# Rotary embedding on one core: slabs of one batch and 16 KB rows in place of slabs of two batches and 32 KB rows

## The chip, the cores and the metric

The kernel runs on one core of a Trainium2 chip. The metric is the device time of one execution in microseconds (us), as the median of several runs. Beside it there is a profile: one execution recorded by the hardware profiler, with every instruction and every DMA packet.

## What is computed

A rotary position embedding. `x` has 16 batches, 512 positions and 1024 columns in float32; the columns are 16 heads of 64, and each head is a first and a second half of 32. `cos` and `sin` have one row of 32 numbers for each position, shared by all batches and heads.

```python
x = x.reshape(batch, seq, num_heads, head_dim)
x1, x2 = x[..., :half_dim], x[..., half_dim:]
rotated = np.concatenate([x1 * cos - x2 * sin,
                          x1 * sin + x2 * cos], axis=-1)
```

32 MB (33.55 million bytes) are read and as many are written.

## The kernel before

**Slabs.** The work is cut into slabs of `nb` = 2 batches, 8 in all. A slab is 4 MB; each of the 128 partitions holds `rpp` = 8 consecutive positions, which are `W` = 8192 float32 numbers, one unbroken row of 32 KB both in HBM and in SBUF. A pool of `slots` = 5 slab buffers holds them. Results are written over the inputs in the same buffer, and the store goes out from there.

**Transfers.** All loads and stores of slabs are issued by SyncE (SP) into one hardware ring, so they are carried out in the order in which SP issues them. `lead` = 4 loads are issued at the start. After that SP's program alternates: the store of slab s (L133), which waits for the last copy of that slab, then the load of slab s+4 (L66), which waits until its buffer is free, that is, until an earlier store has finished. SP works in order: whatever stands behind a waiting instruction waits too. The 16 DMA engines of the core share each transfer by partitions, 8 partitions each; one row of one partition is one packet.

**Tables.** `cos` and `sin` (L77) are loaded on ScalarE's queue onto `SP` = 64 partitions, turned into bf16 by VectorE (L91 to L96), spread to 128 partitions by a matmul with `spread` (L104) and copied out of PSUM (L106). `ss` holds sin and, for the second half, minus sin.

**Compute.** A slab is handled in pieces of `rows` = 2 positions per partition (128 x 2048), 4 pieces to a slab. For each piece ScalarE casts it to bf16 (L115); VectorE forms the two products with the tables (L120, L121); TensorE adds them in PSUM by matmuls with the identity, the second one reading its operand with the halves of each head exchanged (L125, L127), 8 matmuls to a piece; and ScalarE copies the sum over the input in the slab (L132). The three tiles `xb`, `t1`, `t2` have 3 buffers each, the PSUM tile `acc` has 2. The framework orders each engine's instructions and places the waits from the program's data flow, so ScalarE may do casts of later pieces before the copy of an earlier one.

Of the kernel before, what the change touches and what calls it, by code (L numbers as in the profile page):

```python
# [2 lines left out]

# [4 lines left out]


@with_exitstack  # L10
def kernel(
    ctx: ExitStack,
    tc: tile.TileContext,
    x: bass.AP,
    cos: bass.AP,
    sin: bass.AP,
    num_heads: int,
    out: bass.AP,
):
    nc = tc.nc  # L20
    P = nc.NUM_PARTITIONS

    batch, seq, dim = x.shape
    nh = num_heads
    hd = dim // nh
    half = hd // 2
    bf16 = mybir.dt.bfloat16
    f32 = mybir.dt.float32

    nb = 2  # L30
    slots = 5
    lead = 4
    nslabs = batch // nb
    rpp = nb * seq // P
    W = rpp * dim
    SP = seq // rpp
    rows = 2
    PW = rows * dim
    BANK = 512
    hpb = BANK // hd  # L40

    out_flat = out.rearrange("b s h d -> b s (h d)")

    singles = ctx.enter_context(tc.tile_pool(name="singles", bufs=1))
    slabs = ctx.enter_context(tc.tile_pool(name="slabs", bufs=slots))
    tpool = ctx.enter_context(tc.tile_pool(name="tpool", bufs=3))
    psum = ctx.enter_context(tc.tile_pool(
        name="psum", bufs=2, space=bass.MemoryType.PSUM))


    def dram(t, s):
        return bass.AP(tensor=t.tensor, offset=t.offset + s * nb * seq * dim,
                       ap=[[W, P], [1, W]])


    def view(t, offset, *dims):
        return dataclasses.replace(t, offset=t.offset + offset,
                                   ap=[t.ap[0], *[list(d) for d in dims]])


    slab = {}


    def load(s):
        slab[s] = slabs.tile([P, W], f32, tag="slab", name="slab")
        nc.sync.dma_start(out=slab[s], in_=dram(x, s))  # L66


    for s in range(lead):
        load(s)  # L70

    cos_sb = singles.tile([SP, rpp * half], f32, tag="cos_sb")
    sin_sb = singles.tile([SP, rpp * half], f32, tag="sin_sb")
    for t, src in ((cos_sb, cos), (sin_sb, sin)):
        nc.scalar.dma_start(out=t, in_=bass.AP(  # L77
            tensor=src.tensor, offset=src.offset,
            ap=[[rpp * half, SP], [1, rpp * half]]))

    ident = singles.tile([P, P], bf16, tag="ident")
    masks.make_identity(nc, ident)
    spread = singles.tile([SP, P], bf16, tag="spread")
    for g in range(P // SP):
        nc.gpsimd.tensor_copy(out=spread[:, g * SP:(g + 1) * SP],  # L85
                              in_=ident[:SP, :SP])


    cc1 = singles.tile([SP, rpp * hd], bf16, tag="cc1")
    ss1 = singles.tile([SP, rpp * hd], bf16, tag="ss1")  # L90
    nc.vector.tensor_copy(  # L91
        out=cc1, in_=view(cos_sb, 0, (half, rpp), (0, 2), (1, half)))
    sin_rows = view(sin_sb, 0, (half, rpp), (1, half))
    nc.vector.tensor_copy(  # L94
        out=view(ss1, 0, (hd, rpp), (1, half)), in_=sin_rows)
    nc.vector.tensor_scalar_mul(  # L96
        out=view(ss1, half, (hd, rpp), (1, half)), in0=sin_rows, scalar1=-1.0)
    cc = singles.tile([P, rpp * hd], bf16, tag="cc")
    ss = singles.tile([P, rpp * hd], bf16, tag="ss")
    for wide, one in ((cc, cc1), (ss, ss1)):  # L100
        acc = psum.tile([P, PW], f32, tag="acc", name="acc")
        for q in range(0, rpp * hd, BANK):
            n = min(BANK, rpp * hd - q)
            nc.tensor.matmul(view(acc, q, (1, n)), spread, view(one, q, (1, n)),  # L104
                             start=True, stop=True)
        nc.vector.tensor_copy(out=wide, in_=view(acc, 0, (1, rpp * hd)))  # L106

    for s in range(nslabs):
        xs = slab.pop(s)
        for k in range(rpp // rows):  # L110
            xk = view(xs, k * PW, (1, PW))
            xb = tpool.tile([P, PW], bf16, tag="xb")
            t1 = tpool.tile([P, PW], bf16, tag="t1")
            t2 = tpool.tile([P, PW], bf16, tag="t2")
            nc.scalar.copy(out=xb, in_=xk)  # L115

            def tab(t):
                return view(t, k * rows * hd, (hd, rows), (0, nh), (1, hd))

            nc.vector.tensor_mul(out=t1, in0=xb, in1=tab(cc))  # L120
            nc.vector.tensor_mul(out=t2, in0=xb, in1=tab(ss))  # L121
            acc = psum.tile([P, PW], f32, tag="acc")
            for q in range(0, PW, BANK):
                bank = view(acc, q, (1, BANK))
                nc.tensor.matmul(bank, ident, view(t1, q, (1, BANK)),  # L125
                                 start=True, stop=False)
                nc.tensor.matmul(  # L127
                    bank, ident,
                    view(t2, q + half, (hd, hpb), (-half, 2), (1, half)),
                    start=False, stop=True)  # L130

            nc.scalar.copy(out=xk, in_=acc)  # L132
        nc.sync.dma_start(out=dram(out_flat, s), in_=xs)  # L133
        if s + lead < nslabs:
            load(s + lead)


# [1 line left out]
_INS = ['x', 'cos', 'sin', 'num_heads']  # L139
_OUTS = [((16, 512, 16, 64), 'float32')]  # L140

_NUMBERS = {'num_heads': 16}


# [26 lines left out]
```

## Time and profile before

| what | value |
|---|---|
| time, median of 3 runs | 165.12 us (164.91 to 165.26) |
| the profiled execution | time 164.91 us, span 163.1 us |
| granted TensorE clock in it, mean | 0.798 |
| bytes by DMA | 67.29 MB, mean 412 GB/s |
| busy: ScalarE / TensorE / VectorE | 117.3 / 78.8 / 76.0 us |
| slab transfers | 8 loads and 8 stores of 4096 KB |
| issue to landing, median | 30.2 us (loads), 28.9 us (stores) |
| first store handed over by SP / last one | 34.24 us / 139.1 us |

How to read it: the span runs from the first to the last instruction of the profiled execution; the time has a little more, 1.8 us here. Durations of rows come from this one execution. In a row of the groups the first figure is the busy time of all instructions of the group, the second the mean of one in ns, and the last the idle time of the engine ahead of them with what ended it. "SPq" is SP's own instruction queue. The page cuts the span into 40 slices of 4.08 us; digits are tenths of busy time. A transfer counts as landed when all 16 DMA engines have reported.

### The profile page before, as it was taken

How to read it: one execution, taken by the hardware profiler on the slowest of the kernel's cores; microseconds unless marked ns; L12 is line 12 of the kernel's file. 1: busy time of each engine (PE TensorE's matmuls, PEld its weight loads, DVE VectorE, ACT ScalarE, POOL GpSimd, SP SyncE). 2: the span in 40 equal slices, each digit the busy share in tenths (PEclk: the TensorE clock that was granted, in tenths of full speed). 3: DMA queues.
4: the chain of work that ended last, by engine and by line, in shares of the span. 5: the costliest groups of instructions: out<-in, count | busy, mean ns of one | idle time of the engine just before them, and what ended most of it. 6: DMA issues, size and time to landing. Idle time of an engine off the chain costs nothing.

```text
span 163.1 us, 830 instructions
## 1 busy us (share of the span) xinstructions
PE 78.8 (48%) x258; PEld 28.8 (18%) x258; DVE 76.0 (47%) x69; ACT 117.3 (72%) x65; POOL 1.1 (1%) x8
## 2 busy tenths in 40 slices
PE   0001189458918863974199419905990696000000
PEld 0000024112402320331033103301330132000000
DVE  0001699079537755871597069609920991000000
ACT  3006648999899999998997999999789999100000
POOL 2000000000000000000000000000000000000000
PEclk9999999985795997599858956995597599855555
DMA  6999998999999999999999999999999999999980
GB/s 225 426 394 402 466 434 386 466 434 402 482 402 402 498 382 410 482 396 426 450 410 444 442 410 426 450 418 442 426 426 438 426 426 450 418 450 418 434 370 16
DMA packets 2468, 67.29 MB, mean 412 GB/s; under 512 B 288, under 2 KB 416, under 8 KB 416
## 3 DMA queue, kind: packets, MB, share of 16 engines
q1 hardware_dynamic: 2304, 67.11, 96.3%
q10 hardware_dynamic: 160, 0.13, 0.2%
q8 instruction: 2, 0.03, 0.1%
q14 instruction: 2, 0.02, 0.0%
HBM read 33.69 MB, written 33.55 MB: 412 GB/s over the span
## 4 chain that ended last, share of the span: by engine, by line
PE 28%; ACT 24%; issue 14%; DMA 10%; DVE 8%; ACTq 0%; DVEq 0%
PE acc L127 15%; ACT slab L132 15%; PE acc L125 13%; DMA sin_sb<-in_sin_dram 10%; ACT xb L115 10%; DVE t L121 7%; DVE t L120 1%; PE acc L104 0%; ACTq L77 0%; DVE ss L94 0%; DVE ss L96 0%; ACTq L132 0%; DVEq L120 0%; DVE ss L106 0%; ACTq L115 0%
## 5 line engine op out<-in xcount | busy, mean ns | idle before, releaser
L125 PE MATMUL acc<-t,ident 128*128 128x512 bf16 x128 | 59.1, 462 | 34.3 <-DVE t L120 31.0
L115 ACT CAST xb<-slab 128x2048 bf16<-128x2048 f32 x32 | 59.2, 1904 | 13.0 <-DMA slab<-in_x_dram 10.4
L132 ACT COPY slab<-acc 128x2048 f32<-128x2048 f32 x32 | 58.9, 1869 | 6.9 <-PE acc L127 6.7
L127 PE MATMUL acc<-t,ident 128*128 128x512 bf16 x128 | 58.3, 455 | 6.6 <-DVE t L121 6.6
L120 DVE TENSOR_TENSOR t<-xb,cc 128x2048 bf16<-128x2048 bf16 x32 | 39.1, 1221 | 42.1 <-ACT xb L115 42.1
L121 DVE TENSOR_TENSOR t<-xb,ss 128x2048 bf16<-128x2048 bf16 x32 | 39.0, 1219 | 0.0
L127 PEld LDWEIGHTS <-ident 128*128 128x128 bf16 x128 | 14.4, 112 | 56.5 <-issue 48.5
L125 PEld LDWEIGHTS <-ident 128*128 128x128 bf16 x128 | 14.2, 111 | 38.7 <-issue 27.7
L104 PE MATMUL acc<-cc,spread 64*128 64x512 bf16 x1 | 0.6, 582 | 12.7 <-DVE cc L91 12.7
L91 DVE CAST cc<-cos_sb 64x512 bf16<-64x512 f32 x1 | 0.4, 419 | 12.3 <-DMA cos_sb<-in_cos_dram 12.3
L104 PE MATMUL acc<-ss,spread 64*128 64x512 bf16 x1 | 0.6, 583 | 4.7 <-DVE ss L96 4.7
L115 ACT ACT_TABLE_LOAD x1 | 1.3, 1283 | 1.9 <-issue 1.9
L94 DVE CAST ss<-sin_sb 64x256 bf16<-64x256 f32 x1 | 0.3, 285 | 4.8 <-DMA sin_sb<-in_sin_dram 4.8
L104 PEld LDWEIGHTS <-spread 64*128 64x128 bf16 x2 | 0.2, 102 | 12.6 <-issue 10.8
L106 DVE CAST ss<-acc 128x512 bf16<-128x512 f32 x1 | 0.7, 692 | 0.1
L106 DVE CAST cc<-acc 128x512 bf16<-128x512 f32 x1 | 0.7, 676 | 0.0
L85 POOL COPY spread<-ident 64x64 bf16<-64x64 bf16 x2 | 0.4, 230 | 0.1
masks.py:199 POOL TENSOR_SCALAR_AFFINE_SELECT ident<-ident 128x128 bf16<-128x128 bf16 x1 | 0.3, 292 | 0.1
L96 DVE TENSOR_SCALAR ss<-sin_sb 64x256 bf16<-64x256 f32 x1 | 0.3, 278 | 0.0
masks.py:197 POOL MEMSET ident<- 128x128 bf16 x1 | 0.2, 205 | 0.3 <-POOLq L152 0.3
L152 POOL MEMSET const-bfloat16-1.0<- 128x1 bf16 x1 | 0.1, 101 | 0.0
L152 POOL MEMSET const-uint8-127<- 128x1 uint8 x1 | 0.1, 101 | 0.0
(2 smaller groups left out, 0.2 us busy)
## 6 DMA issues: line engine op xcount, KB each, us to landing
slab<-in_x_dram SPq DMA_DIRECT2D x8, 4096.0 KB, 30.2
out_dram<-slab SPq DMA_DIRECT2D x8, 4096.0 KB, 28.9
cos_sb<-in_cos_dram ACTq DMA_DIRECT2D x1, 64.0 KB, 11.5
sin_sb<-in_sin_dram ACTq DMA_DIRECT2D x1, 64.0 KB, 16.2
```

What stands on the lines that cost most here:

```text
L85: nc.gpsimd.tensor_copy(out=spread[:, g * SP:(g + 1) * SP], in_=ident[:SP, :SP])
L91: nc.vector.tensor_copy(out=cc1, in_=view(cos_sb, 0, (half, rpp), (0, 2), (1, half)))
L94: nc.vector.tensor_copy(out=view(ss1, 0, (hd, rpp), (1, half)), in_=sin_rows)
L96: nc.vector.tensor_scalar_mul(out=view(ss1, half, (hd, rpp), (1, half)), in0=sin_rows, scalar1=-1.0)
L104: nc.tensor.matmul(view(acc, q, (1, n)), spread, view(one, q, (1, n)), start=True, stop=True)
L106: nc.vector.tensor_copy(out=wide, in_=view(acc, 0, (1, rpp * hd)))
L115: nc.scalar.copy(out=xb, in_=xk)
L120: nc.vector.tensor_mul(out=t1, in0=xb, in1=tab(cc))
L121: nc.vector.tensor_mul(out=t2, in0=xb, in1=tab(ss))
L125: nc.tensor.matmul(bank, ident, view(t1, q, (1, BANK)), start=True, stop=False)
L127: nc.tensor.matmul(bank, ident, view(t2, q + half, (hd, hpb), (-half, 2), (1, half)), start=False, stop=True)
L132: nc.scalar.copy(out=xk, in_=acc)
```

## The change

Three numbers change; the rest follows from them.

```diff
-    nb = 2
-    slots = 5
-    lead = 4
+    nb = 1
+    slots = 9
+    lead = 6
     nslabs = batch // nb
     rpp = nb * seq // P
     W = rpp * dim
```

There are 16 slabs of one batch, 2 MB each. A partition holds 4 positions, a row of 16 KB. Nine buffers of 16 KB take 144 KB of a partition, where five of 32 KB took 160. Six loads are issued at the start, so the load of slab s+6 follows the store of slab s in SP's program, and it waits for the store of slab s-3, whose buffer it takes. A slab has 2 pieces instead of 4; pieces and their instructions keep their shapes. The tables lie on 128 partitions with 4 positions each, the spreading matrix is the 128 x 128 identity, and the two spreading matmuls have 256 columns instead of 512. SP still issues all loads and stores of slabs into the same ring.

## The prediction

> **What bounds the kernel now.** I read the page's busy shares first, then its slices, then the queue table, then the waits of SP's queue, and last the single packet records of the trace. The busiest engine is ScalarE:
>
> ```profile
> PE 78.8 (48%) x258; PEld 28.8 (18%) x258; DVE 76.0 (47%) x69; ACT 117.3 (72%) x65; POOL 1.1 (1%) x8
> ...
> ACT  3006648999899999998997999999789999100000
> ...
> DMA  6999998999999999999999999999999999999980
> GB/s 225 426 394 402 466 434 386 466 434 402 482 402 402 498 382 410 482 396 426 450 410 444 442 410 426 450 418 442 426 426 438 426 426 450 418 450 418 434 370 16
> ```
>
> ScalarE stops at slice 35 and all compute is over 24 us before the span's end, while the DMA row stays at 8 or 9 from the second slice to the last but one. Nothing that compute does sets the end; bytes do.
>
> ```profile
> q1 hardware_dynamic: 2304, 67.11, 96.3%
> q10 hardware_dynamic: 160, 0.13, 0.2%
> ...
> HBM read 33.69 MB, written 33.55 MB: 412 GB/s over the span
> ```
>
> Queue 1 is SP's ring: 16 transfers of 4 MB, each 128 rows of 32 KB plus 16 small completion packets, so 16 x 144 = 2304. In the packet records a 32 KB packet takes 1.213 us in the median, and successive ones on one DMA engine start 1.210 us apart: there are no holes. Each of the 16 engines must move 128 of them: 128 x 1.210 = 154.9 us. The first starts at 1.76 us; most engines end near 159.0, the slowest at 161.8, and the span ends at 163.1.
>
> ```profile
> SPq L133 <- ACT slab L132: 92.9, 7, 20.6
> SPq L66 <- DMA out_dram<-slab: 28.0, 3, 15.7
> SPq L166 <- DMA out_dram<-slab: 22.6, 1, 22.6
> ```
>
> SP's own waits (us in total, times, longest) look large, but while SP waits its ring is full of earlier transfers. The last row is the end itself: SP waits 22.6 us for stores that had long been handed over. The chain of waits breaks off at the last ScalarE copy (139 us) and does not show this; the DMA row does.
>
> **The change part by part.** Against the profiled execution: span 163.1, time 164.91, so 1.8 lie outside the span. The median of the runs, 165.12, is 0.2 above it, and I add the differences to the median.
>
> *Bytes and the compute.* The bytes stay. The 32 casts, 32 copies, 64 products and 256 matmuls keep their shapes, since `rows` stays at 2. The tables become 128 x 256 instead of 64 x 512 and the two spreading matmuls get half as wide; this lies in the first 19 us, off the DMA engines' path. Nothing here.
>
> *Twice as many, half as long packets.* 16 KB rows make 256 data packets per engine for 128. What one packet costs beside its bytes: the 1 KB table packets took 46 ns, the 32 KB ones 1213; the line through both is 27.2 GB/s and 8.4 ns fixed. But packets overlap by 3 to 4 ns: a 1 KB packet holds its ring back by 40 ns, 2.5 more than its bytes; a 32 KB one by 1210, 5 more than its 1204.7. So 128 extra packets cost 128 x 2.5 = 0.3 us to 128 x 9 = 1.15 us. I take 5 ns, from the row of the same queue: **+0.64**. Nothing hides it, because the engines have no holes.
>
> *Sixteen more transfers.* Each ends with a 9 ns completion packet on each engine. Across such a packet the gap between data packets is +2 ns in the median, against -4 without: 6 ns x 16 = **+0.1** (0.05 to 0.2). The Trainium skill speaks against the change here: "DMA: Bandwidth & Descriptors" (Anatomy of one DMA) gives every DMA a fixed 2.0 us beside its bytes; laid end to end, 16 more would be 32 us and the time some 197. The gap of 2 ns says that this cost lies beside the next transfer's packets while the ring is full. The same page (Why small descriptors are slow) gives 3 cycles per packet; at its 850 MHz that is 3.5 ns, between the ends that the rows give, and would be an estimate of 0.45 us for the packets in place of my term.
>
> *More changes of direction.* Once loads and stores alternate, an engine goes from one to the other: 9 times now (from load 3 to store 0 up to load 7 to store 4), 21 times after. Between 39 and 145 us the packets' excess over 1.213 us is 0.60 us per engine in the mean, bunched where one direction follows the other (near 41, 51, 60, 80, 100, 119). 0.60 / 9 x 12 = **+0.8**. Bounds: nothing, if the excess belongs to the start of each 4 MB of a direction and halves with it; and, for an engine that lags, much more. Following the slowest engine's packets by their times (not unique everywhere), I find long ones of 1.72, 1.77, 1.68, 1.90 and 1.35 us: 2.35 us over, 0.26 per change, so up to 3.1.
>
> *Start and tables.* The first packets took 1.56 to 2.42, a mean excess of 0.70 us: access time, which I leave (-0.35 if it goes with the size). A table needs 8 packets of 512 B per engine for 4 of 1 KB, alternating with slab packets half as long: sin should still come near 17.5 us. Twice as many disturbances of slab packets (0.32 us of excess up to 17.6 us): **+0.1** (0 to 0.35).
>
> *Six small loads ahead instead of four large: does the ring run dry?* Before, the four loads fed the ring up to about 43 us and the first store was issued at 34.2:
>
> ```profile
> 34.24 0.35 SPq L133 DMA_DIRECT2D out_dram<-slab  x1
> 34.63 0.43 SPq L66 DMA_DIRECT2D slab<-in_x_dram  x1
> ```
>
> After, six loads hold as many bytes as three did, so the ring is fed up to 13.6 (the first cast, on the first load's landing) + 2 x 9.7 (8 packets of 1.210 per engine) = 33.0. The first store now waits for two copies, not four. These are the rows:
>
> ```profile
> 24.88 1.87 ACT L132 COPY slab<-acc 128x2048 f32<-128x2048 f32 x1 [1.25 <-PE acc L127]
> ...
> 27.02 3.63 ACT L132 COPY slab<-acc 128x2048 f32<-128x2048 f32 x2 [0.27 <-PE acc L127]
> ```
>
> The second copy ends at 28.9, so store 0 and load 6 go out at about 29, 4 us before the ring would be empty. Later the margin grows: a slab's store and a load feed the ring for 2 x 4.85 = 9.7 us, and ScalarE needs 2 x (1.90 + 1.87) = 7.5 per slab. A load now waits for the store three slabs back: load s+6 takes the slot of slab s-3 behind store s on SP. That store comes before about six transfers, 29 us of work, in the same ring, so store s+1 queued behind this wait has cover. If the cover goes, each us of delay is a us of time. Cost: nothing.
>
> Sum: 0.64 + 0.1 + 0.8 + 0.1 = 1.6 us, so 165.12 + 1.6 = **166.7 us**. Bounds: 0.3 + 0.05 + 0 - 0.35 = 0.0 and 1.15 + 0.2 + 3.1 + 0.35 = 4.8.
>
> **The rivals.** *Faster: the lagging engine is relieved.* The end belongs to one engine, 2.8 us behind the middle of the others. For: on what looks like that engine, an instruction fetch of 16 KB takes 1.00 us at 60.4 us, and the slab packet behind it 1.72; a second fetch at 122.4 (1.00, then 1.58) adds to some engine. 16 KB at 27.2 GB/s need 0.6, so 2 x 0.4 are lost in the fetches and 0.51 + 0.37 in the packets behind. If a blocked slab packet half as long loses half, and the long packets at the changes of direction shrink alike, the lag falls from 2.8 to 1.4. This decides when packets and changes cost under 1.4 together. With the low packet cost of 0.3, completions 0.1 and tables 0.1 and no cost of changes: 165.12 - 1.4 + 0.5 = 164.2. Against: twice as many packets meet the fetches and changes.
>
> *No change.* The excess at a change halves with the transfer, and fixed costs overlap down to the 2.5 ns row: +0.3 for packets, less what the start saves: 165.1 to 165.4. For: the 2 ns gap shows how well the engines overlap. Against: the 5 ns of the same queue's own packets.
>
> *Slower by more: the ring dries up at the start.* If ScalarE, freed by earlier landings, does three more casts before the copies of slab 0 (the trace shows it doing three in a row at 13.6), store 0 comes 3 x 1.90 = 5.7 us later, at 34.7: a hole of 1.7 and a new start of about 1, on top of the sum: 165.12 + 1.6 + 2.7 = 169.4. Against: ScalarE waited for the tables then, not for slabs, and has only three buffers to cast into.
>
> **How the numbers follow.** A measurement of this kernel can tell a change of about 0.2%, 0.33 us. The forecast (packets and changes of direction, 165.5 to about 169) gets 0.60, the dry ring 0.08, no change 0.13, the relieved engine 0.19. So faster 0.19, same 0.13, slower 0.68. The range from 164.4 to 168.9 leaves out half of the dry ring, a little of the fastest case and the forecast's upper tail. The forecast's own range is 165.5 to 168.9.
>
> **What would show it.** Queue 1 with 32 x 144 = 4608 packets and as many bytes; 16 KB packets that start 0.607 to 0.610 us apart (0.605 or less would make the packet term nothing); no slice of the DMA row under 8 between the first and the last two; the first store near 29 us; the last store handed over near 139 and the rest pure DMA. Packet excess where loads and stores alternate of about 1.4 us per engine instead of 0.60. The prediction is wrong if the DMA row shows a hole near 33 us, if the engines' ends draw closer together than 2.8 us, or if the excess per change falls to half.

## The result and the profile after

The changed kernel takes 179.3 us (median of 4 runs, 178.47 to 179.91) against 165.18 us: a ratio of 1.0855, 95% interval 1.0808 to 1.0901. The profiled execution took 178.47 us with a span of 176.7 us, 13.6 us more than before. The forecast had the sign right, but 166.7 us and a range up to 168.9. In one experiment below, one of two executions was markedly slower than the other (194.0 us beside 188.5), and only the faster one is used.

On the page of the changed kernel, the rows of ScalarE and of the DMA engines (40 slices, now of 4.42 us) and the queue table:

```profile
ACT  2074799999998869195691873929647469294430
...
DMA  6999999999999999999999999999999987428055
...
q1 hardware_dynamic: 4608, 67.11, 89.9%
```

The DMA row is full up to slice 32, about 142 us, as before. Then it falls to 4 and 2 and even to 0: near the end of the program the ring is empty, and the DMA engines wait for work. ScalarE, which was done by slice 35 before, now works to the last slices, with holes from slice 15 on. SP's queue shows the same. Its columns are start, duration, queue and line, transfer, count:

```profile
101.33 0.34 SPq L133 DMA_DIRECT2D out_dram<-slab  x1
101.76 0.73 SPq L66 DMA_DIRECT2D slab<-in_x_dram  x1
112.47 57.31 SPq L133 DMA_DIRECT2D out_dram<-slab  x6
```

The last six stores go out over 57 us, the last one at 169.4 us. Before, the last store was handed over at 139.1 us. In the waits of SP's queue, the store's wait for ScalarE has grown and the final wait has shrunk:

```profile
SPq L133 <- ACT slab L132: 145.2, 16, 15.3
SPq L166 <- DMA out_dram<-slab: 5.9, 1, 5.9
```

The final wait was 22.6 us, the sign of a ring with much left in it. It is now 5.9 us, one store of 2 MB and its reporting. The end is set by the last copy on ScalarE, not by bytes.

Why ScalarE is late is seen in its timeline (start, time, instruction, count, idle time before it and what ended it). First the kernel before, from its fifth slab on:

```profile
77.44 7.30 ACT L115 CAST xb<-slab 128x2048 bf16<-128x2048 f32 x4
84.97 1.86 ACT L132 COPY slab<-acc 128x2048 f32<-128x2048 f32 x1 [0.23 <-PE acc L127]
87.78 3.63 ACT L132 COPY slab<-acc 128x2048 f32<-128x2048 f32 x2 [0.94 <-PE acc L127]
91.67 1.86 ACT L132 COPY slab<-acc 128x2048 f32<-128x2048 f32 x1 [0.26 <-PE acc L127]
93.43 7.30 ACT L115 CAST xb<-slab 128x2048 bf16<-128x2048 f32 x4
```

Then the changed kernel, from its eighth slab on:

```profile
66.81 3.70 ACT L115 CAST xb<-slab 128x2048 bf16<-128x2048 f32 x2
74.39 3.79 ACT L132 COPY slab<-acc 128x2048 f32<-128x2048 f32 x2 [3.88 <-PE acc L127]
78.08 3.70 ACT L115 CAST xb<-slab 128x2048 bf16<-128x2048 f32 x2
85.66 3.63 ACT L132 COPY slab<-acc 128x2048 f32<-128x2048 f32 x2 [3.88 <-PE acc L127]
```

In both, the framework's order puts all casts of a slab before its copies, and the casts of the next slab behind them. From the first cast of a slab to its first copy the way leads through VectorE and TensorE, and it takes as long in both: 84.97 - 77.44 = 7.53 us and 74.39 - 66.81 = 7.58 us. Before, four casts (7.30 us) fill this time. Now there are only two (3.70 us), and ScalarE stands idle for 3.5 to 3.9 us in every slab. A period is 78.08 - 66.81 = 11.3 us per 2 MB, where the kernel before has (93.43 - 77.44) / 2 = 8.0. A store and a load of 2 MB take 9.7 us in the ring. So ScalarE had been quicker than the ring and is now slower, for nine slabs.

The next slab's data were not missing: the load of the ninth slab had landed by about 64.7 us, and its casts began at 78.08.

The way is not of one length: it is longer where TensorE's granted clock is low. The PEclk row of the page gives the clock that was granted to TensorE in each slice, in tenths; below it stand an earlier cast of the changed kernel and the copy of the same piece:

```profile
PEclk9999999889879996597985856969758589695675
...
55.37 1.90 ACT L115 CAST xb<-slab 128x2048 bf16<-128x2048 f32 x1
...
61.48 1.86 ACT L132 COPY slab<-acc 128x2048 f32<-128x2048 f32 x1 [0.64 <-PE acc L127]
```

In slices 13 and 14, with the clock at 9 (90% or more), the way took 61.48 - 55.37 = 6.11 us. The block at 66.81 us fell into slices 16 and 17, with 6 and 5 tenths. Its matmuls started 0.43 us apart up to 74.5 us and 0.22 us after. In all nine slabs a part of the way fell into such a stretch, and the way took 7.2 to 7.6 us. With a way of 6.1 us the period would be, as an estimate, 6.1 + 2 x 1.8 = 9.7 us, just what the ring needs. The mean clock is not what differs (0.817 here, 0.798 before), and the blocks of the kernel before ran at the low clock as well, but under four casts. No run separates the order from the clock that went with it.

### The profile page after: what moved, and what is told of

It reads as the page before. It is cut to its first block, busy times and chain, and to the rows that moved or that the text cites. A ratio compares the mean times of both kernels' runs of the same rounds, so it can differ in the third digit from the quotient of the medians.

```text
span 176.7 us, 857 instructions
## 1 busy us (share of the span) xinstructions
PE 84.0 (48%) x258; PEld 29.9 (17%) x258; DVE 75.6 (43%) x69; ACT 117.7 (67%) x65; POOL 1.0 (1%) x7
## 3 DMA queue, kind: packets, MB, share of 16 engines
q1 hardware_dynamic: 4608, 67.11, 89.9%
## 5 line engine op out<-in xcount | busy, mean ns | idle before, releaser
L125 PE MATMUL acc<-t,ident 128*128 128x512 bf16 x128 | 62.1, 485 | 59.4 <-DVE t L120 56.2
L127 PE MATMUL acc<-t,ident 128*128 128x512 bf16 x128 | 60.5, 473 | 10.2 <-DVE t L121 10.2
L127 PEld LDWEIGHTS <-ident 128*128 128x128 bf16 x128 | 15.1, 118 | 82.6 <-issue 75.5
L125 PEld LDWEIGHTS <-ident 128*128 128x128 bf16 x128 | 14.6, 114 | 45.5 <-issue 35.9
```

What stands on the lines that cost most here:

```text
L125: nc.tensor.matmul(bank, ident, view(t1, q, (1, BANK)), start=True, stop=False)
L127: nc.tensor.matmul(bank, ident, view(t2, q + half, (hd, hpb), (-half, 2), (1, half)), start=False, stop=True)
```

## The experiments

The first pair swaps the order of ScalarE's queue and nothing else. In both kernels the same loop issues the pieces, and each cast or copy on ScalarE is tied to the one before it; the list says how many casts precede each copy. In the kernel with small slabs it is the order of the kernel before:

```diff
+    ahead = [4, 4, 4, 5, 7, 8, 8, 9, 11, 12, 12, 13, 15, 16, 16, 16,
+             20, 20, 20, 20, 24, 24, 24, 24, 28, 28, 28, 28, 32, 32, 32, 32]
...
+    def act(ins):
+        if order:
+            tc.add_manual_dep(ins.ins, order[-1].ins.name, mybir.DependencyInfo(
+                mybir.DependencyClass.NoSync, mybir.DependencyReason.DATA),
+                reason="order")
+        order.append(ins)
...
+    for p in range(npieces):
...
+        while done < ahead[p]:
+            cast(done)
+            done += 1
...
+        act(nc.scalar.copy(out=xk, in_=acc))
```

**Small slabs, order of before.** Expected:

> The changed kernel (slabs of one batch, nine slots, six loads ahead) with ScalarE's casts and copies held in the order that the kernel before had. Theory ORDER (the new order of ScalarE's queue, two casts then two copies of one slab, sets a period of 11.2 us per slab): ScalarE is as quick as before, its last copy ends near 140 us, the DMA engines are full to the end, and the time is 165.2 us plus the 1.6 us of the recorded sum, 166 to 168 us. Theory GRAIN (2 MB transfers, 16 KB rows or nine slots cost the time): still 178 to 180 us.

Measured: 165.84 us, ratio to the kernel before 1.0052 (1.0038 to 1.0066). Of the 14 us, 13 are gone, with 16 KB rows, nine slots and six loads ahead all in place. The rows of ScalarE and of the DMA engines on its page:

```profile
ACT  3084499999999999989989499961969839660000
...
DMA  5999999999999999999999999999999999999991
```

Its last load and its last six stores in the timeline of SP's queue:

```profile
99.18 0.33 SPq L66 DMA_DIRECT2D slab<-in_x_dram  x1
101.59 45.02 SPq L157 DMA_DIRECT2D out_dram<-slab  x6
```

The DMA row has no hole, ScalarE is done by slice 36, and the last store goes out at 146.3 us. That is later than the 140 us that ORDER expected, with the ring still full, and the time is just under its range. GRAIN falls.

**Large slabs, order of the changed kernel.** The same loop in the kernel before, with the other list:

```diff
+    ahead = [4, 4, 5, 5, 6, 8, 9, 9, 10, 12, 12, 13, 14, 14, 16, 16,
+             18, 18, 20, 20, 22, 22, 24, 24, 26, 26, 28, 28, 30, 30, 32, 32]
```

> The kernel before (slabs of two batches, five slots, four loads ahead) with ScalarE's casts and copies held in the order that the changed kernel has. Theory ORDER: from the thirteenth piece on 11.2 us for two pieces; the last copy ends near 169 us as in the changed kernel, and a last store of 4 MB (9.7 us) stands behind it: 181 to 185 us. Theory GRAIN: 165 to 166 us, as before.

Measured: 188.5 us, in a single execution. So the order alone makes the large slabs slow as well. The DMA row of its page:

```profile
DMA  6989998999998999999999999999890029700595
```

And ScalarE's timeline in its middle:

```profile
95.57 3.70 ACT L127 CAST xb<-slab 128x2048 bf16<-128x2048 f32 x2
102.77 3.63 ACT L155 COPY slab<-acc 128x2048 f32<-128x2048 f32 x2 [3.50 <-PE acc L150]
106.29 3.71 ACT L127 CAST xb<-slab 128x2048 bf16<-128x2048 f32 x2
113.87 1.86 ACT L155 COPY slab<-acc 128x2048 f32<-128x2048 f32 x1 [3.87 <-issue]
```

The idle times of 3.5 to 3.9 us are there with 4 MB slabs too. It is slower than I had expected, and 10.0 us slower than the profiled execution of the changed kernel. The last copy ends at 174.6 us, not at 169.4 (5.2 later, since the first 4 MB load lets the first cast start at 13.9 us instead of 8.6), and the final wait behind it is 10.7 us, not 5.9 (4.8 more). I had left the first of the two out.

**Ten slots, eight loads ahead.** The framework's own order, one edit in the changed kernel:

```diff
-    slots = 9
-    lead = 6
+    slots = 10
+    lead = 8
```

> The changed kernel with ten slots and eight loads ahead, the same bytes ahead and the same buffer space as before; ScalarE's order left to the framework, which now puts two casts before two copies from the ninth slab on instead of the seventh. Theory ORDER: two slabs fewer at 11.2 us instead of about 7.5, so the last copy 5 to 8 us earlier and 171 to 175 us. Theory GRAIN: 178 to 180 us if small transfers are it; 165 to 167 us if it was the bytes ahead that were lacking.

Measured: 170.67 us, ratio 1.0343 (1.0313 to 1.0374). The change to two casts, a hole and two copies comes at 81.87 us instead of 66.81, and there are 7 such groups, not 9:

```profile
81.87 3.70 ACT L115 CAST xb<-slab 128x2048 bf16<-128x2048 f32 x2
89.46 3.77 ACT L132 COPY slab<-acc 128x2048 f32<-128x2048 f32 x2 [3.88 <-PE acc L127]
93.12 3.70 ACT L115 CAST xb<-slab 128x2048 bf16<-128x2048 f32 x2
```

The gain of 8.6 us is a little over what two slabs were expected to give. The border moved by as many slabs as `lead` did. Together with the swap of the orders this suggests that the depth of the loads acts on the time through the order that the framework derives from it. Why it derives this order was not tried.

**Small slabs, casts ahead.** The same loop, with three casts in front and then one copy and one cast in turn:

```diff
+        while done < min(p + 3, npieces):
+            cast(done)
+            done += 1
```

> The changed kernel with ScalarE's queue held in the order: three casts, then one copy and one cast in turn, across the borders of the slabs. Theory ORDER: with a cast of a later piece in front of every copy, ScalarE needs about 2 x (1.90 + 1.87) = 7.5 us per slab, never sets the end, and the time is that of the DMA engines, 165.4 to 166.5 us, as with the order of before (165.84). If another thing of the small slabs held the changed kernel up and the order of before only hid it, 170 us or more.

Measured: 165.54 us, ratio 1.0038 (1.0014 to 1.0061). A second order without the hole gives the same time, so the order of before has no merit of its own.

**Transfers alone.** Two kernels leave out all computation and the tables; the loop only stores what was loaded:

```diff
     for s in range(nslabs):
...
-        nc.sync.dma_start(out=dram(out_flat, s), in_=xs)
+        nc.sync.dma_start(out=dram(out_flat, s), in_=slab[s])
         if s + lead < nslabs:
             load(s + lead)
```

> Leaves out all computation and the tables: slabs of two batches are loaded and stored again, same ring, slots and loads ahead as before. It measures the transfers alone. 128 packets of 1.210 us and a first one late by 0.7 make 1.8 + 154.9 + 0.7 = 157.4, some 0.5 for changes of direction and 1.5 at the end: span 159 to 160, time 160.5 to 162 us; lower than the kernel before by the instruction fetches that hit one DMA engine. If the lag of one engine has another cause, 163 to 165 us.

> The same with slabs of one batch, nine slots and six loads ahead. Theory ORDER: the grain of the transfers costs what is left between small and large slabs under one order (0.9 us): 0.5 to 1.2 us over the kernel with large slabs. Theory GRAIN: 10 us over it or more.

Measured: 164.12 us with large slabs (ratio to the kernel before 0.9937, 0.9912 to 0.9963) and 165.25 us with small ones (1.0014, 0.9994 to 1.0034). The difference, 1.1 us, is the price of the smaller grain by itself. But the large ones miss the expectation by 2 us or more:

```profile
DMA  6999999999699999999999999999999999999991
...
DMA packets 2304, 67.11 MB, mean 414 GB/s; under 512 B 256, under 2 KB 256, under 8 KB 256
...
q1 hardware_dynamic: 2304, 67.11, 97.2%
```

No queue but that of the slabs appears: there is not one instruction fetch while the slabs move. Still the slowest engine ends at 161.0 us, 2 us behind the middle of the others (158.9). In the packet records the excess over 1.213 us from 39 to 140 us is 1.39 us per engine, above the 0.60 of the kernel before. So the lag of one engine, on which my rival for a gain rested, exists without the fetches.

**Large slabs, fewer matmuls.** With casts ahead, VectorE adds the products of every second piece and writes the slab, instead of TensorE and ScalarE:

```diff
+        if p % 2 == 0:
...
+        else:
+            halves = ((hd, PW // hd), (half, 2), (1, half))
+            nc.vector.tensor_tensor(
+                out=view(xk, 0, *halves), in0=view(t1, 0, *halves),
+                in1=view(t2, half, (hd, PW // hd), (-half, 2), (1, half)),
+                op=mybir.AluOpType.add)
```

> Slabs of two batches as before, casts ahead as in the first of these kernels, and in every second piece VectorE adds the two products and writes the slab itself, in place of 8 matmuls and a copy: half of TensorE's instructions, so that TensorE needs one fetch of 16 KB or none instead of two while the DMA engines are full. VectorE's add is estimated at 1.2 to 2.5 us, which makes 98 to 118 us busy on VectorE, under the DMA's 155. If the end belongs to the engine that the fetches hit, 162.5 to 164.3 us; if not, 164.5 to 165.5 us, as before.

Measured: 164.53 us, ratio 0.9968 (0.9952 to 0.9983). The group of the new instruction in the groups by line:

```profile
L158 DVE TENSOR_TENSOR slab<-t,t 128x2048 f32<-128x2048 bf16 x16 | 36.6, 2286 | 0.2
```

And the queue of the 16 KB fetches on its page, which had 2 packets before:

```profile
q8 instruction: 1, 0.02, 0.0%
```

To tell whether the order or the fewer matmuls did it, both were run side by side:

> The kernel before with casts ahead of the copies and all matmuls kept, to tell whether the order or the fewer matmuls took 0.5 us off in the kernel with fewer matmuls. ScalarE does not set the end in the kernel before, so the order alone gives nothing: 164.8 to 165.3 us, and the 0.5 us belong to the fewer instructions. If the order is what helped, 164.3 to 164.7 us.

> The kernel with fewer matmuls once more beside it on the same chip: 164.2 to 164.9 us, 0.3% under the kernel before.

Measured: casts ahead alone 164.99 us, ratio 0.9997 (0.9985 to 1.0009); fewer matmuls again 164.63 us, 0.9977 (0.9962 to 0.9992). So the order gives nothing where ScalarE is not what sets the end, and one addition on VectorE for 8 matmuls and a copy, in every second piece, gives 0.2 to 0.3%. This is the quickest version found, ahead of both kernels and 0.4 to 0.5 us above the transfers alone. One fetch of 16 KB less, as its trace shows, is not shown to be the cause: 164.53 us lies in the range expected if the end does not belong to the engine that the fetches hit, and in the profiled executions the slowest DMA engine ended 2.6 and 2.7 us behind the middle of the others with one fetch, against 2.8 and 3.1 with two (the kernel before, casts ahead alone), so most of its lag stays. What gives the 0.2 to 0.3% stays open.

## Why the prediction was wrong

**The step that failed** is the one that asked whether the ring runs dry: "Later the margin grows: ... ScalarE needs 2 x (1.90 + 1.87) = 7.5 per slab", at a cost of nothing. This took ScalarE's busy time for its pace. After the first seven slabs the pace was 11.3 us, because the instructions of a slab stood in one block and the way through VectorE and TensorE was no longer covered. The swap of the orders shows both halves: without the hole 165.84 us, with it 188.5 us even with large slabs. The ring's 9.7 us lie between the two paces, so the step sat just where the sign turns. That the kernel became slower, as forecast, is luck: the terms on which the forecast rested come to 0.9 of the 14.1 us.

**It could have been read off before.** Rows of the kernel before show four casts in one block, 7.30 us, then a copy 0.23 us later: the block of casts was just long enough to cover a way of 7.53 us. If the framework keeps such blocks, halving the slab halves the block and leaves the way: 7.53 + 2 x 1.8 gives 11.1 us per slab. I had looked at the first slabs alone, where the casts of the next slab stand among the copies. The total of the idle rows hid it, since 7 us in all looked like no hole.

**The rival of a dry ring** had the mechanism, ScalarE's order letting the ring run empty, but at the wrong end. At the start the cover was better than thought: store 0 went out at 24.05 us, not 29, because the first 2 MB let the casts begin at 8.58 us. The hole came from 143 us on, when the loads were all done and the stores came one per 11 us. The size agrees: as far as the packets' times tell the DMA engines apart, three were busy without a break up to 152 us. Such an engine shows two holes, about 5.9 us there and 7.1 us at 163, and without these 13.0 us its end at 175.2 would be at 162.2, where the small slabs under the old order end.

**The terms of the sum**, tested by the small slabs under the old order, come to 0.9 us (165.84 against 164.92) instead of 1.6; the excess figures are from one profiled execution of each:

- Packets: 4608 of them, 16 KB ones starting 607 ns apart. Two of them less one of 32 KB, 1209 to 1210 ns, leave 4 to 5 ns, times 128 = 0.5 to 0.6 us, where 0.64 was forecast. Right.
- Changes of direction: the excess from 39 to 140 us rose from 0.60 to 0.73 us per engine, +0.13 where +0.8 was forecast. This term was mis-sized by six: with 21 changes for 9 it hardly grows, and in the transfers alone it fell from 1.39 to 0.75 us, so it does not go by their number. The lower bound, nothing, was near the truth.
- Start and tables: up to 39 us the excess rose from 1.09 to 1.19 us; +0.1 was right.
- Completions: where a completion packet lies between two slab packets, they mostly start 613 ns apart, 6 more; times 16 that is 0.1 us, as forecast.

The fixed cost of a DMA that the Trainium skill states ("DMA: Bandwidth & Descriptors", Anatomy of one DMA: some 2 us each) did not show: 16 more transfers cost 0.9 us with computation and 1.1 without, 0.06 to 0.07 each with their packets, in a ring that is always full. That section is on DMAs issued from GpSimd, and these are issued from SP. The weighing was right on this point, and it drew my attention to the transfers and away from ScalarE's queue.

**No change and the relieved engine.** The 0.9 us of the small slabs under the old order are more than "no change" allowed. Their slowest engine ended at 162.2 us, 2.6 us behind the middle of the others, where before it was 161.8 and 2.8, so the lag did not fall to 1.4. And it does not need the fetches.

## What to carry to other kernels

When a block of work is made smaller, ask of each in-order engine what covers the way through the other engines, and read it where the kernel is in its steady state: the time from the first instruction of a block to the first one that needs its result, against the work that stands between them in the queue. An engine that is 72% busy and off the end of the path can become the bound by its order alone, without a single instruction more. Slab size, slots and loads ahead, changed together, changed the order that the scheduling framework picked here; compare the order of the queues before comparing transfers, and fix it by hand if it must hold.

## What was not expected of the hardware

Transfers alone are hardly quicker than the kernel before: 164.12 us for 67.1 MB through one ring with 32 KB rows, against 165.06. In the one with large slabs 16 packets, as many as there are engines, took 1.8 to 2.1 us near 40 us, about when the first loads gave way to stores, and one engine ended 2 us late without any fetch. TensorE's fetches of 16 KB came when it had started 183 to 197 and again 429 to 453 of its weight loads and matmuls, in every kernel with 32 pieces of matmuls. They lie 232 to 266 apart, which agrees with the blocks of 256 instructions that the Trainium skill states ("Runtime: NRT & Kernel Launch", Instruction fetch mechanics). Each took 0.92 to 1.19 us beside the slabs' packets.
